# Norms of two heads in one transfer, last head sums split two slots sooner, x added to two output rows in their second phase

## The chip, the cores and the metric

The kernel runs on one core of a Trainium2 chip. The metric is the time of one execution on the device in microseconds; the median of three runs before the change is 1361.49 us (1359.12 to 1362.36). TensorE (PE) multiplies matrices into PSUM banks, VectorE (DVE), ScalarE (ACT) and GpSimd (POOL) work on tiles in SBUF, and SyncE (SP) issues nearly all DMA transfers, which 16 DMA engines carry out. Every engine takes its own instructions in order; semaphores hold one engine until another is done.

## The reference

One layer with two token mixers side by side, for 2048 positions and a model width of 1024, all in float32. The input is normalised and projected once; the projection's six parts feed a gated short convolution (8 heads of 128) and a gated linear recurrence (16 heads of 64). Each head's output is RMS-normalised, multiplied by a SiLU gate, and one output projection and the residual follow.

```python
xn = rms_norm(h, ln_g)
proj = jnp.einsum('bsd,de->bse', xn, w_in)
...
y_conv = headwise_rms_norm(y_conv, N_CONV_HEADS, conv_out_g) * jax.nn.silu(g_conv)
...
y_lru = headwise_rms_norm(y_lru, N_LRU_HEADS, lru_out_g) * jax.nn.silu(g_lru)
y = jnp.concatenate([y_conv, y_lru], axis=-1)
h = h + jnp.einsum('bse,ed->bsd', y, w_out)
return rms_norm(h, final_g)
```

## The kernel before

**Tiles and steps.** The two large products are cut into steps; the table `steps` (line 255) is their order. Steps 0 to 47 are projections of kind `l` (recurrence), `a` and `b` (convolution) for the first half of the positions (h = 0) and the second (h = 1). Steps 48 to 63 are the output projection, kind `o`: phase 0 multiplies the recurrence's heads, phase 1 the convolution's, and each phase has eight tiles m, one for two blocks of 128 rows (rows 2m and 2m + 1). So step 48 + m is phase 0 of tile m and step 56 + m is phase 1 of tile m.

A step computes a 2 x 2 block product with Winograd's variant of Strassen: seven products of sums of blocks. A float32 operand is split into a high part that the fast matmul takes exactly and a low remainder, and each product is three matmuls per block (high x high, high x low, low x high). A step has seven slots (eight where the set of the other operand changes), and a slot has 12 matmuls of 128 x 512 on TensorE. Line 924 is the matmul.

**What sets the order.** The program's order is written by hand. `at(slots, f)` puts f into a list, and `tick()`, called at the start of each slot, runs what has come due: `at(2, f)` runs f two ticks later. The order in which these functions are called is the order of the instructions on each engine. `prep` brings the pieces of the next step's plan, one or two a slot, and `load_next` starts the loads of the step after the next, in slot 3.

**The operands of the output steps.** The gated outputs of the heads lie in DRAM (`yd`), not yet normalised; the norms, one over the root of each head's mean square, lie in DRAM too (`rsd[0]` and `rsd[1]`, one for each half of the positions). `load_z` (line 269) loads four pieces `raw` of `yd`, loads the matching norms into `zr`, broadcast over partitions, and multiplies the two on VectorE. In phase 0 a tile of 128 partitions holds two heads of 64, so the norms of each 64 partitions come from another row, with a transfer of its own (line 285); in phase 1 one row serves all 128 (line 282). From a step that is planned this way, `s_plan` makes sums of the four pieces (VectorE), casts them (ScalarE) and takes the remainders (VectorE).

For four output tiles this is done long before, by the generator `jobs` (line 340), which runs one piece a slot beside the projections of h = 1 and stores the finished operands in DRAM (`so`); when their steps come, they are only loaded (`s<-so`). These are the first two tiles of each phase.

**The head sums.** `finish` (line 617) multiplies gain and gate, stores the product to `yd`, squares the ungated output and calls `head_sums`, in slots counted from the step's last part. After the last head of a half, `head_norms` (line 567) copies the sums to `rt` and its remainder (`split`, ScalarE and VectorE), adds the sums over partitions with four matmuls (`add`, tile `norm_ps`), takes the root (`root`, tile `hn`) and stores the norms in `rsd` (`store`).

**The output.** `outp` (line 837) collects a tile's products in two rows `ob`. In phase 0 it loads the rows of x into `xr`, adds `ob` and stores the sum in DRAM (`od`). In phase 1 it loads `od` back into `xr`, adds, takes the final norm and stores `out`. PSUM has five banks for these products; a bank is free when `q`, `u`, `rr` or `ob` has been copied out of it.

**The queues.** SP issues the transfers in the program's order, and a transfer that waits holds all behind it. Each carries one of a small number of semaphores in turn, so it also waits for an earlier transfer that used the same one.

Of the kernel before, what the change touches and what calls it, by code (L numbers as in the profile page):

```python
# [38 lines left out]
def hymba_kernel(ctx: ExitStack, tc: tile.TileContext, x, xt, w_in, par, lamc, w_gate, w_out, final_g, out):  # L39
# [215 lines left out]
    steps = [(kind, 0, k) for k in range(KT) for kind in "lab"]  # L255
    steps += [(kind, 1, k) for kind, k in zip("lablab", (0, 1, 1, 1, 0, 0))]
    steps += [(kind, 1, k) for k in range(2, KT) for kind in "lab"]
    steps += [("o", ph, m) for ph in range(2) for m in range(KT)]
    cols = {"l": (GLX, GLG), "a": (GC, GX), "b": (GB, GG)}

    def set_of(n):
# [7 lines left out]
    def load_z(h, m, zr, wait):  # L269
        r = [piece("raw") for _ in range(4)]  # L270
        fs = []
        for i in range(2):
            c, b = divmod(2 * m + i, NB)
            assert normed[c // 2]
            rs_ = rsd[c // 2][c % 2]
            zz_, zq_ = [], []
            z2 = wt(("u", "r")[i], "zr") if zr else None

            def norms(dst, k0, n):
                dst = dst.rearrange("p (k t) -> p k t", k=n)  # L280
                if h == 1:
                    nc.sync.dma_start(dst, rs_[b:b + 1, k0:k0 + n, :].broadcast_to((P, n, P)))
                else:
                    for w in range(2):
                        nc.sync.dma_start(dst[w * 64:w * 64 + 64], rs_[b:b + 1, k0 + w * KT:k0 + w * KT + n, :]
                                          .broadcast_to((64, n, P)))

            for q in range(2):
                zz = r[2 * i + q].rearrange("p (k t) -> p k t", k=NB)
                zq = z2[:, q * C:(q + 1) * C] if zr else piece("zr")  # L290
                k0 = (1 - h) * KT + q * NB
                nc.sync.dma_start(zz, yd[c][b, :, k0:k0 + NB, :])
                if not zr:
                    norms(zq, k0, NB)
                elif q == 1:
                    norms(z2, (1 - h) * KT, KT)
                zq = zq.rearrange("p (k t) -> p k t", k=NB)
                fs.append(lambda zz=zz, zq=zq: tt(zz, zz, zq, ALU.mult))
        if wait is not None:
            for i in range(2):  # L300
                at(max(wait + i, 1), *fs[2 * i:2 * i + 2])
        return r, fs
# [19 lines left out]
    def hl_done(n):  # L322
        hlc[0] -= n
# [15 lines left out]

    def jobs():  # L340
        tjobs = [(t, j) for t in (2, 3) for j in range(NB)]
        for ph, m in ((0, 0), (0, 1), (1, 0), (1, 1)):
            (a11, a12, a21, a22), fs = load_z(ph, m, False, None)
            yield from (None,) * 4
            for f in fs[:2]:
                f()
            yield
            for f in fs[2:]:
                f()
            yield  # L350
            if m:
                x_ = aux("s3")
                tt(x_, a11, a21, ALU.subtract)
                tt(a21, a21, a22, ALU.add)
            b = {}

            def blocks():
                if tjobs:
                    b[0] = tjobs.pop(0)
                    b[1] = [piece("traw") for _ in range(4)]  # L360
                    for p, src in zip(b[1], w_blocks(*b[0])):
                        nc.sync.dma_start(p, src)

            def sums():
                if b:
                    b11, b12, b21, b22 = b[1]
                    tt(b11, b12, b11, ALU.subtract)
                    tt(b12, b22, b12, ALU.subtract)

            def more():  # L370
                if b:
                    b11, b12, b21, b22 = b[1]
                    tt(b22, b22, b11, ALU.subtract)
                    tt(b21, b21, b22, ALU.subtract)
                    to = td[b[0]]
                    at(1, lambda: [nc.sync.dma_start(to[n], v) for n, v in enumerate((b22, b11, b12, b21))])
                    b.clear()

            blocks()
            prev = None  # L380
            nothing = lambda: None
            if m:
                items = [(0, a11, lambda: tt(a11, a21, a11, ALU.subtract)), (3, x_, nothing), (2, a21, nothing),
                         (1, a11, nothing), (4, a12, lambda: tt(a12, a12, a11, ALU.subtract)),
                         (6, a22, nothing), (5, a12, nothing)]
            else:
                items = [(n, v, nothing) for n, v in enumerate((a12, a22, a11, a21))]
            for n, (i, v, after) in enumerate(items):
                if prev:
                    prev()  # L390
                    prev = None
                while not may():
                    yield
                t, = hl_tile("so")
                nc.scalar.copy(t[:, 0:C], v)

                def prev(t=t, i=i, v=v, after=after, dst=so[ph, m]):
                    tt(t[:, C:2 * C], v, t[:, 0:C].bitcast(F32), ALU.subtract)
                    after()
                    at(2, lambda: nc.sync.dma_start(  # L400
                        dst[i], t.bitcast(F32).rearrange("p (h c) -> p h c", h=2)))
                    at(3, lambda: hl_done(1))

                yield
            prev()
            made.add((ph, m))
            sums()
            yield
            more()
            yield  # L410
            yield
            blocks()
            yield from (None,) * 4
            sums()
            yield
            more()
            yield from (None,) * 2
# [149 lines left out]
    def head_norms(h):  # L567
        sm_ = sums[0]
        rt, = hl_tile("rt")
        rh, rl = rt[:, 0:C], rt[:, C:2 * C]  # L570
        at(6, lambda: hl_done(1))
        v = {}

        def split():
# [23 lines left out]
            normed[h] = True  # L598

        split()  # L600
        at(3, add)
        at(4, root)
        at(5, lambda: nc.vector.reciprocal(out=v["rs"], in_=v["rs"]))
        at(5, store)

    def head_sums(h, kt, y):
        if summed[0] == 0:
# [4 lines left out]
        summed[0] += 1  # L612
        if summed[0] == 2 * KT:
            summed[0] = 0
            at(1 if h else 7, lambda: head_norms(h))

    def finish(d0, h, kt, y, sil, gain):
        def f1():
# [191 lines left out]
    def conv_b(h, k):  # L810
        g = wt("o2", "gb", bufs=O2)

        def put(which, bank, other):
# [12 lines left out]
                combine(g[:, 0:C] if which == 21 else g[:, C:N2], bank, other)  # L826
            if which == 21:
                silu(g)
                finish(6, h, k, t, g, pt[:, CG + k:CG + k + 1])

        return put

# [4 lines left out]
    def outp(ph, m):  # L837
        ob = [wt("hl", "ob", bufs=HL) for _ in range(2)]
        xr, rest = {}, []
        if ph == 1 and m == 0:  # L840
            fg[0] = wt("t", "fg")
            nc.sync.dma_start(fg[0], final_g.rearrange("(o d) -> o d", o=1).broadcast_to((P, D)))

# [2 lines left out]
            xr[i] = wt("ig", "xr", bufs=IG) if i == 0 else wt("o2", "xr", bufs=O2)  # L846
            nc.sync.dma_start(xr[i], x[tb * P:(tb + 1) * P, :] if ph == 0 else od[tb])

        last = ph == 1 and m == KT - 1
        at(2 if last else 5, lambda: load(0))  # L850
        at(2 if last else 6, lambda: load(1))

        def fin(i):
            tb = 2 * m + i
            if ph == 0:
                at(1, lambda: tt(xr[i], xr[i], ob[i], ALU.add))
                at(3, lambda: nc.sync.dma_start(od[tb], xr[i]))
                return
# [436 lines left out]
```

## Time and profile before

| what | value |
|---|---|
| median of three runs | 1361.49 us |
| the profiled execution's own time | 1361.65 us |
| its span, from the first to the last instruction | 1359.8 us |
| TensorE busy | 1301.9 us |
| VectorE busy | 1032.5 us |
| ScalarE busy | 748.4 us |
| mean DMA rate over the span | 261 GB/s |
| mean granted TensorE clock | 0.989 |

A row of the profile names line, engine and operation, then output tile <- input tiles with their shapes, and how many such instructions there are. In rows in order of time, the first number is the start in us, the second the duration of the group, and a bracket at the end the idle time of the engine before it and what ended it. SPq rows are issues of transfers; their duration is that of the issuing. A row of the waits gives the sum in us, the number of times and the longest. The view of stretches of time gives, for each, the busy time of each engine, the granted clock, the mean busy share of the 16 DMA engines and the rate that they moved. A list of transfers gives their count and the KB of each.

In the profile's clock the output steps start at 1024.5 us (step 48); steps 50, 56 and 63 start at 1072.8, 1191.0 and 1330.4 us.

### The profile page before, as it was taken

To read this page: it belongs to the slowest core of one execution; us is meant where nothing else is said; L and a number is where in the kernel's file an instruction comes from. 1 tells how busy PE (TensorE), PEld (TensorE's weight loads), DVE (VectorE), ACT (ScalarE), POOL (GpSimd) and SP (SyncE) were. 2 spreads that over 40 slices of the span, in tenths; PEclk is the share of its full clock that TensorE was granted. 3 is DMA by queue.
4 is the path that set the end of the run, shared out by engine and by line. 5 is a ranking of instruction groups with operands and counts; after the bars stand their busy time and mean duration, and the time that the engine had idled before them with its cause. 6 is when DMAs were issued, how large, how long until landed. Compare 5 with 4: busy or idle time off the path is not lost.

```text
span 1359.8 us, 16618 instructions
## 1 busy us (share of the span) xinstructions
PE 1301.9 (96%) x5648; PEld 1058.6 (78%) x5648; DVE 1032.5 (76%) x1245; ACT 748.4 (55%) x1139; POOL 226.2 (17%) x160
## 2 busy tenths in 40 slices
PE   6989999999999999899999999999999799998997
PEld 5867877777878787777888888888878688887886
DVE  7778788789989897978566676667458776759885
ACT  7475757575665757565544645364456233444443
POOL 3204242333334340101010110101000000000000
PEclk9989999999999999999999999999999899999999
DMA  7137797988879888542789999999778889797643
GB/s 284 31 119 258 270 252 273 278 296 302 319 281 330 291 291 304 173 162 79 247 304 286 335 354 331 332 339 365 228 253 313 249 236 227 271 404 260 240 146 136
DMA packets 158805, 355.28 MB, mean 261 GB/s; under 512 B 17920, under 2 KB 52736, under 8 KB 158720
## 3 DMA queue, kind: packets, MB, share of 16 engines
q1 hardware_dynamic: 158432, 353.90, 77.1%
q8 instruction: 45, 0.74, 0.2%
q14 instruction: 40, 0.33, 0.1%
q10 hardware_dynamic: 288, 0.32, 0.1%
HBM read 217.11 MB, written 137.04 MB: 260 GB/s over the span
## 4 chain that ended last, share of the span: by engine, by line
PE 40%; DMA 7%; DVE 4%; ACT 3%; issue 1%; SPq 0%; DVEq 0%; ACTq 0%
PE bank L924 40%; DMA traw<-td 1%; DMA zr<-rsd 1%; PE gate L704 1%; ACT i L711 1%; ACT r L711 1%; DVE tl L163 1%; DMA traw<-in_w_out_dram 1%; DMA od<-xr 1%; DMA xr<-od 1%; DVE s L163 1%; DMA xr<-in_x_dram 1%; ACT th L435 1%; DMA yd<-gl 0%; DMA raw<-yd 0%
## 5 line engine op out<-in xcount | busy, mean ns | idle before, releaser
L924 PE MATMUL bank<-th,s 128*128 128x512 f32 x3632 | 1138.8, 392 | 19.9 <-ACT u L1232 10.0
L924 PEld LDWEIGHTS bank<-th,s 128*128 128x128 f32 x3632 | 686.1, 189 | 173.5 <-ACT u L1232 15.0
L924 PE MATMUL bank<-tl,s 128*128 128x512 f32 x1816 | 711.1, 392 | 1.6 <-DVE tl L163 1.3
L924 PEld LDWEIGHTS bank<-tl,s 128*128 128x128 f32 x1816 | 343.2, 189 | 74.8 <-DVE tl L163 3.5
L163 POOL TENSOR_TENSOR s<-raw,s 128x512 fp32r<-128x512 f32 x62 | 110.2, 1790 | 253.9 <-ACT s L200 210.7
L200 ACT CAST s<-raw 128x512 fp32r<-128x512 f32 x140 | 84.5, 616 | 75.4 <-PE bank L924 41.8
L163 DVE TENSOR_TENSOR tl<-traw,th 128x512 fp32r<-128x512 f32 x117 | 85.1, 763 | 40.4 <-ACT th L435 30.0
L1232 ACT COPY u<-bank 128x512 f32<-128x512 f32 x58 | 34.0, 586 | 145.6 <-PE bank L924 77.8
L163 DVE TENSOR_TENSOR s<-s,s 128x512 fp32r<-128x512 f32 x105 | 95.5, 909 | 10.5 <-ACT s L200 10.5
L163 POOL TENSOR_TENSOR gb<-gb,sg 128x1024 f32<-128x1024 f32 x16 | 40.6, 2537 | 348.3 <-ACT sg L637 328.2
L163 DVE TENSOR_TENSOR s<-raw,s 128x512 fp32r<-128x512 f32 (+1 forms) x125 | 92.7, 765 | 6.5 <-ACT s L982 4.4
L200 ACT CAST s<-s 128x512 fp32r<-128x512 f32 x105 | 64.7, 616 | 30.3 <-DVE s L163 25.8
L435 ACT CAST th<-traw 128x512 fp32r<-128x512 f32 x96 | 55.1, 618 | 30.7 <-DMA traw<-td 17.8
L1229 ACT COPY q<-bank 128x512 f32<-128x512 f32 x58 | 33.9, 584 | 68.0 <-PE bank L924 59.2
L678 DVE SCALAR_TENSOR_TENSOR u<-xl,pt,u 128x1024 f32<-128x1024 f32 x48 | 62.7, 1306 | 6.3 <-ACT u L674 5.7
L163 DVE TENSOR_TENSOR raw<-raw,zr 128x512 f32<-128x512 f32 x64 | 41.2, 684 | 34.6 <-DMA zr<-rsd 31.1
L1235 ACT COPY rr<-bank 128x512 f32<-128x512 f32 x58 | 33.8, 583 | 50.4 <-PE bank L924 50.4
L788 DVE SCALAR_TENSOR_TENSOR t<-p,pt,t 128x1024 f32<-128x1024 f32 x32 | 46.5, 1454 | 5.9 <-ACT t L785 5.1
L163 DVE TENSOR_TENSOR st<-u,st 64x1024 fp32r<-64x1024 f32 x32 | 46.5, 1452 | 1.0
L711 ACT ACTIVATE r<-gate,pt 64x512 f32<-64x512 f32 x64 | 43.8, 684 | 3.1 <-PE gate L704 2.4
L163 POOL TENSOR_TENSOR gl<-gl,sg 128x1024 f32<-128x1024 f32 x16 | 40.4, 2523 | 24.5 <-ACT sg L637 24.5
L711 ACT ACTIVATE i<-gate,pt 64x512 f32<-64x512 f32 x64 | 43.8, 684 | 1.1
(153 smaller groups left out, 1153.7 us busy)
## 6 DMA issues: line engine op xcount, KB each, us to landing
sd<-s SPq DMA_DIRECT2D x151, 512.0 KB
s<-sd SPq DMA_DIRECT2D x151, 512.0 KB
raw<-in_w_in_dram SPq DMA_DIRECT2D x104, 256.0 KB
raw<-yd SPq DMA_DIRECT2D x64, 256.0 KB
traw<-in_w_out_dram SPq DMA_DIRECT2D x64, 256.0 KB
so<-so SPq DMA_DIRECT2D x22, 512.0 KB
s<-so SPq DMA_DIRECT2D x22, 512.0 KB
yd<-gl SPq DMA_DIRECT2D x32, 256.0 KB
```

What stands on the lines that cost most here:

```text
L163: (eng or nc.vector).tensor_tensor(out=out, in0=a, in1=b, op=op)
L200: nc.scalar.copy(dst[i][0], val(i))
L435: nc.scalar.copy(self.dst[i, j][0], self.r[i, j])
L678: nc.vector.scalar_tensor_tensor(out=v["u"], in0=o1[:, 1 + j:1 + j + N2], scalar=lw[j], in1=v["u"], op0=ALU.mult, op1=ALU.add)
L704: nc.tensor.matmul(ps[j], v["gw"][n][:, j, :], v["st"][j][:, sl], start=(n == 0), stop=(n == 1))
L711: nc.scalar.activation(out=g_[hi, sl], in_=v["ps"][j][src], func=AF.Sigmoid, bias=pt[src, bias + k:bias + k + 1])
L788: nc.vector.scalar_tensor_tensor(out=tcur["t"], in0=p[:, 2 + j:2 + j + N2], scalar=cw[j], in1=tcur["t"], op0=ALU.mult, op1=ALU.add)
L924: nc.tensor.matmul(bank, a[:, js], b, start=start and n == 0, stop=stop and n == 2, skip_group_check=more)
L1229: nc.scalar.copy(q1, bk["A"])
L1232: nc.scalar.copy(u2, bk["A"])
L1235: nc.scalar.copy(rr, bk["A"])
```

## The change

There are three parts.

1. In `load_z`, the norms of the two heads of a phase 0 tile come with one transfer in place of two. Its DRAM side counts the two heads, then 64 copies, then the row. This holds for steps 50 to 55 (two transfers a step, 512 KB each) and for the tiles (0,0) and (0,1) in `jobs` (four each, 256 KB each).
2. For the second half of the positions, the last `finish` runs a slot sooner and `head_norms` another slot sooner; inside `head_norms` the later parts (`add`, `root`, `store`) are put two slots later, so that they keep their slots.
3. In phase 0 the tiles 0 and 1 store `ob` in `od` without x. In phase 1 these two tiles run last, and their rows of x are loaded there (`xo`) and added to `xr` ahead of `ob`. `jobs` prepares tiles (1,2) and (1,3) in place of (1,0) and (1,1).

```diff
-    steps += [("o", ph, m) for ph in range(2) for m in range(KT)]
+    steps += [("o", 0, m) for m in range(KT)]
+    steps += [("o", 1, m) for m in (2, 3, 4, 5, 6, 7, 0, 1)]
+    X_LATE = (0, 1)
...
-                    for w in range(2):
-                        nc.sync.dma_start(dst[w * 64:w * 64 + 64], rs_[b:b + 1, k0 + w * KT:k0 + w * KT + n, :]
-                                          .broadcast_to((64, n, P)))
+                    src = rs_[b].rearrange("(w k) t -> w k t", k=KT)[1:3, k0 - KT:k0 - KT + n, :]
+                    nc.sync.dma_start(dst, src.unsqueeze(1).broadcast_to((2, 64, n, P)))
...
-        for ph, m in ((0, 0), (0, 1), (1, 0), (1, 1)):
+        for ph, m in ((0, 0), (0, 1), (1, 2), (1, 3)):
...
-        at(6, lambda: hl_done(1))
+        d = 2 if h else 0
+        at(6 + d, lambda: hl_done(1))
...
-        at(3, add)
-        at(4, root)
-        at(5, lambda: nc.vector.reciprocal(out=v["rs"], in_=v["rs"]))
-        at(5, store)
+        at(3 + d, add)
+        at(4 + d, root)
+        at(5 + d, lambda: nc.vector.reciprocal(out=v["rs"], in_=v["rs"]))
+        at(5 + d, store)
...
-            at(1 if h else 7, lambda: head_norms(h))
+            at(0 if h else 7, lambda: head_norms(h))
...
-                finish(6, h, k, t, g, pt[:, CG + k:CG + k + 1])
+                finish(5 if h and k == KT - 1 else 6, h, k, t, g, pt[:, CG + k:CG + k + 1])
...
+        def row(i):
+            xo = wt("o1", "xo", n=N2 + 4)[:, 0:D]
+            tb = 2 * m + i
+            nc.sync.dma_start(xo, x[tb * P:(tb + 1) * P, :])
+            return lambda: tt(xr[i], xr[i], xo, ALU.add)
...
-        last = ph == 1 and m == KT - 1
-        at(2 if last else 5, lambda: load(0))
-        at(2 if last else 6, lambda: load(1))
+        last = ph == 1 and m == 1
+        if ph == 1 and m in X_LATE:
+            add = []
+            order = (1, 0) if last else (0, 1)
+            at(1, lambda: rows(add, order[0]))
+            at(2, lambda: load(order[1]))
+            at(3 if last else 4, lambda: (add[0](), add.append(row(order[1]))))
+            at(5 if last else 7, lambda: add[1]())
+        elif ph == 1 or m not in X_LATE:
+            at(5, lambda: load(0))
+            at(6, lambda: load(1))
...
+            if ph == 0 and m in X_LATE:
+                at(2, lambda: nc.sync.dma_start(od[tb], ob[i]))
+                return
```

Two places show what moves. The first is SP's queue at steps 48 and 49: the loads of step 50 (`raw`, `zr`), then those of step 51, the stores of the last gated rows (`gb`) and of the first output rows (`od`). Before:

```order
L226 DMA s<-so_119 128x1024
L847 DMA xr<-in_x_dram 128x1024
L492 DMA traw<-td_128 128x512
L492 DMA traw<-td_129 128x512
L292 DMA raw<-yd_85 128x512 x2
L285 DMA zr<-rsd_88 64x1024 x2
L292 DMA raw<-yd_85 128x512 x2
L285 DMA zr<-rsd_88 64x1024 x2
L226 DMA s<-so_119 128x1024
```

After the change the same stretch of the queue reads:

```order
L226 DMA s<-so_119 128x1024
L493 DMA traw<-td_128 128x512
L493 DMA traw<-td_129 128x512
L293 DMA raw<-yd_85 128x512 x2
L287 DMA zr<-rsd_88 128x1x1024
L293 DMA raw<-yd_85 128x512 x2
L287 DMA zr<-rsd_88 128x1x1024
L626 DMA yd_86<-gb 128x4x128
L626 DMA yd_87<-gb 128x4x128
L226 DMA s<-so_119 128x1024
```

The load of x is gone from it (another one, a few rows above, too), each pair of norms of 64 rows is one transfer of 128 rows, and the two stores of `gb` stand ahead of the next `s`. A little later in the same queue, at steps 50 and 51, the norms of the second half (`rsd_89`) are stored and the loads of step 52 follow. Before:

```order
L847 DMA xr<-in_x_dram 128x1024 x2
L595 DMA rsd_89<-hn 8x8x32 x12
L857 DMA od_136<-xr 128x1024
L292 DMA raw<-yd_86 128x512 x2
L285 DMA zr<-rsd_89 64x1024 x2
L292 DMA raw<-yd_86 128x512 x2
```

With the change:

```order
L597 DMA rsd_89<-hn 8x8x32 x12
L876 DMA od_136<-ob 128x1024
L876 DMA od_137<-ob 128x1024
L293 DMA raw<-yd_86 128x512 x2
L287 DMA zr<-rsd_89 128x1x1024
L293 DMA raw<-yd_86 128x512 x2
```

Two loads of x are gone, and the second store of tile 1's rows (`od_137`) now stands ahead of step 52's loads. The second place is VectorE at steps 48 and 49, where `sums` become `rt` and step 50's pieces are multiplied. Before:

```order
L163 TENSOR_TENSOR xr<-xr,ob 128x1024
L163 TENSOR_TENSOR tl<-traw,th 128x512 x4
L609 TENSOR_REDUCE sums<-t 128x32
L163 TENSOR_TENSOR raw<-raw,zr 128x512 x2
L163 TENSOR_TENSOR xr<-xr,ob 128x1024
L163 TENSOR_TENSOR tl<-traw,th 128x512 x2
L163 TENSOR_TENSOR raw<-raw,zr 128x512 x2
L163 TENSOR_TENSOR rt<-sums,rt 128x512
```

With the change:

```order
L163 TENSOR_TENSOR tl<-traw,th 128x512 x6
L611 TENSOR_REDUCE sums<-t 128x32
L163 TENSOR_TENSOR rt<-sums,rt 128x512
L163 TENSOR_TENSOR tl<-traw,th 128x512 x2
L163 TENSOR_TENSOR raw<-raw,zr 128x512 x2
L163 TENSOR_TENSOR tl<-traw,th 128x512 x2
L163 TENSOR_TENSOR raw<-raw,zr 128x512 x2
```

`rt` now stands ahead of both pairs of products with `zr`, and the two adds of x and `ob` are gone.

More of the change, by code (lines that the diff above doesn't have):

```diff
@@ L350, in jobs @@
             yield
-            if m:
+            if m % 2:
                 x_ = aux("s3")
@@ L381, in jobs @@
             nothing = lambda: None
-            if m:
+            if m % 2:
                 items = [(0, a11, lambda: tt(a11, a21, a11, ALU.subtract)), (3, x_, nothing), (2, a21, nothing),
@@ L839, in outp @@
         xr, rest = {}, []
-        if ph == 1 and m == 0:
+        if ph == 1 and m == 2:
             fg[0] = wt("t", "fg")
@@ L847, in load, with rows @@
             nc.sync.dma_start(xr[i], x[tb * P:(tb + 1) * P, :] if ph == 0 else od[tb])
-        last = ph == 1 and m == KT - 1
-        at(2 if last else 5, lambda: load(0))
-        at(2 if last else 6, lambda: load(1))
+        def row(i):
[3 more added lines that the diff above has]
+            return lambda: tt(xr[i], xr[i], xo, ALU.add)
+        def rows(first, i):
+            load(i)
+            first.append(row(i))
+        last = ph == 1 and m == 1
[9 more added lines that the diff above has]
+            at(6, lambda: load(1))
         def fin(i):
             tb = 2 * m + i
+            if ph == 0 and m in X_LATE:
+                at(2, lambda: nc.sync.dma_start(od[tb], ob[i]))
+                return
             if ph == 0:
```

## The prediction, made before the changed kernel was run

> **What bounds the kernel now.** I read the page first, then TensorE's waits, the slices of time around the largest of them engine by engine, and last the DMA views.
>
> ```profile
> span 1359.8 us, 16618 instructions
> ...
> PE 1301.9 (96%) x5648; PEld 1058.6 (78%) x5648; DVE 1032.5 (76%) x1245; ACT 748.4 (55%) x1139; POOL 226.2 (17%) x160
> ```
> ```profile
> PE bank L924 <- ACT u L1232: 10.0, 10, 3.8
> ...
> PE norm_ps L582 <- DVE rt L163: 7.1, 1, 7.1
> ```
>
> TensorE is busy for 96% of the span, so a change can win only what is left of its pauses. The largest pause that this change touches is 7.1 us long and happens once: the matmuls of the last head sums wait for `rt`, which VectorE writes. The other row names the second way in which TensorE is held, a copy of `u` by ScalarE. The neighbourhood of the pause, in time:
>
> ```profile
> 1057.14 0.28 PE L582 MATMUL norm_ps<-rt,sel 128*96 128x256 f32 x1
> 1064.53 0.95 PE L582 MATMUL norm_ps<-rt,sel 128*96 128x256 f32 x3 [7.11 <-DVE rt L163]
> ...
> 1066.13 1.05 PE L924 MATMUL bank<-th,s 128*128 128x512 f32 x2
> ...
> 1070.52 0.62 PE L924 MATMUL bank<-th,s 128*128 128x512 f32 x2
> ```
> ```profile
> 1058.12 1.29 DVE L163 TENSOR_TENSOR raw<-raw,zr 128x512 f32<-128x512 f32 x2 [5.38 <-DMA zr<-rsd]
> ...
> 1062.58 1.29 DVE L163 TENSOR_TENSOR raw<-raw,zr 128x512 f32<-128x512 f32 x2 [0.82 <-DMA zr<-rsd]
> 1063.79 0.68 DVE L163 TENSOR_TENSOR rt<-sums,rt 128x512 fp32r<-128x512 f32 x1
> ```
> ```profile
> 1065.88 0.62 ACT L200 CAST s<-s 128x512 fp32r<-128x512 f32 x1 [6.41 <-DVE s L163]
> 1066.40 0.58 ACT L1232 COPY u<-bank 128x512 f32<-128x512 f32 x1
> ```
>
> VectorE takes its work in order. `rt` stands behind two pairs of products raw*zr of step 50, and these wait for the norms `zr` from DRAM. After the pause two matmuls take 1.05 us where they later take 0.62, for about ten matmuls: 2 us more. The pause costs 9 us. The last two rows matter for what comes after it: the copy of `u`, which frees a PSUM bank, stands on ScalarE behind a cast that needs the same products. So the norms' arrival, not `rt` alone, sets the pace here, and the DMA engines are full:
>
> ```profile
> core 0: us, PE busy (x) PEld busy (x) DVE busy (x) ACT busy (x) POOL busy (x), PEclk, DMA share, GB/s
> 714.00:782.00 68.00, 67.78 (x298) 55.49 (x298) 42.89 (x49) 36.73 (x48) 5.91 (x4) 1.00 0.92 310
> 1044.00:1048.00 4.00, 4.00 (x19) 3.34 (x18) 1.55 (x4) 2.68 (x4) 0.00 (x0) 1.00 1.02 374
> 1054.00:1056.00 2.00, 2.00 (x11) 1.59 (x9) 0.00 (x0) 0.69 (x2) 0.00 (x0) 1.00 1.01 224
> 1058.00:1062.00 4.00, 0.00 (x0) 0.00 (x0) 3.63 (x5) 0.62 (x1) 0.00 (x0) 0.67 1.04 234
> 1064.00:1067.00 3.00, 2.47 (x8) 2.08 (x9) 2.97 (x6) 1.11 (x2) 0.00 (x0) 0.50 1.04 422
> 1216.00:1218.00 2.00, 2.00 (x11) 1.65 (x10) 1.09 (x2) 1.27 (x4) 0.00 (x0) 1.00 1.08 398
> ```
>
> All these stretches have a DMA share around 1. Plain transfers of 128 rows move 422 GB/s, 26.4 GB/s for each of 16 engines; the stretches full of the 64-row norms move 224 to 234.
>
> **The transfers of norms: how many engines carry one.** This is the part on which my number rests. Each pair of 64-row transfers becomes one, whose DRAM side counts 2 heads, then 64 copies, then the row; its SBUF side counts 128 rows. The trace shows no such form, but it shows what the leading count does:
>
> ```profile
> DMA packets 158805, 355.28 MB, mean 261 GB/s; under 512 B 17920, under 2 KB 52736, under 8 KB 158720
> ...
> sd<-s SPq DMA_DIRECT2D x151, 512.0 KB
> ...
> rsd<-hn SPq DMA_DIRECT2D x24, 8.0 KB
> ...
> pt<-in_par_dram ACTq DMA_DIRECT2D x1, 52.0 KB
> rsx<-rs SPq DMA_DIRECT2D x2, 2.0 KB
> lam<-in_lam_dram SPq DMA_DIRECT2D x1, 4.0 KB
> ```
>
> The view lists 956 transfers, from the first of these rows to the last. Data pieces under 512 B are few: 24 x 64 of 128 B for `rsd`, 2 x 512 of 4 B for `rsx`, 128 rows each of `pt` and `lam`: 2,816. The other 15,104 small packets belong to no data. They are 16 for each of 932 transfers and 8 for each of the 24 with 8 leading rows: 14,912 + 192 = 15,104, exactly. I read them as one end mark per engine used: 128 and 64 leading rows use 16 engines, 8 use 8. Continued to a leading 2 against 128, an equal cut of both sides gives **2 engines**. The bounds of a 512 KB transfer are then 524,288 / (2 x 26.4) = 9.9 us and 524,288 / 422 = 1.24 us. I take 9.9, because both counts seen obey the same rule.
>
> The Trainium skill, DMA: Bandwidth & Descriptors, section "Why a DMA increments its semaphore by 16 and not by 1", says that the engines of a transfer are the largest number up to 16 that divides both sides' slowest dimension, and that they are always the lowest-numbered ones. The count above agrees for 8, 64 and 128; no run here shows 2. By that page this change's norms would all queue on the same two engines, as the sum below has it.
>
> **The sum at the output steps.** Norms are loaded this way for steps 50 to 55, two transfers each. Every other transfer has a sixteenth of its bytes on each of those two engines and queues there behind the norms (1.24 us for 512 KB, 0.62 for 256).
>
> ```profile
> 1040.93 1.36 SPq L226 DMA_DIRECT2D s<-so  x1
> 1042.38 0.39 SPq L847 DMA_DIRECT2D xr<-in_x_dram  x1
> ...
> 1044.38 0.44 SPq L847 DMA_DIRECT2D xr<-in_x_dram  x1
> ...
> 1157.85 0.32 SPq L857 DMA_DIRECT2D od<-xr  x1
> ```
> ```profile
> 1073.17 1.29 DVE L163 TENSOR_TENSOR raw<-raw,zr 128x512 f32<-128x512 f32 x2 [4.61 <-DMA zr<-rsd]
> ...
> 1078.44 1.22 DVE L163 TENSOR_TENSOR raw<-raw,zr 128x512 f32<-128x512 f32 x2
> ...
> 1083.25 0.69 DVE L163 TENSOR_TENSOR ob<-bank,u 128x512 f32<-128x512 f32 x1
> ...
> 1154.19 1.29 DVE L163 TENSOR_TENSOR raw<-raw,zr 128x512 f32<-128x512 f32 x2 [1.40 <-DMA zr<-rsd]
> ...
> 1159.07 0.68 DVE L163 TENSOR_TENSOR ob<-bank,u 128x512 f32<-128x512 f32 x1
> ```
>
> The `s` load issued at 1040.93 leaves the busy engines near 1043.5. Without the two loads of x, what follows up to step 50's second norms is four `td` halves and one `s` (3.7 us), then twice (two `yd` halves 1.24 + norms 9.9): 22.3; done at 1069.5. Then 6.2 us of `gb`, `s`, `od` and step 51's 22.3: its second norms land at about 1098.5, and the products that began at 1078.44 begin 20 us later.
>
> From there each step repeats. Step 52's loads stand in SP's queue behind `od_137`, which needs `ob<-bank,u`: 4.8 + 0.7 us after those products begin, 1104.0. With 2 us for issue and landing (my estimate: at the end of the run the last 256 KB store shows 3.9 us from issue to the end of the span), 1.24 for `od` and 22.3, step 52 lands at 1129.5. For steps 53 to 55 SP waits for the `od` behind the products: 1157.85 - 1154.19 = 3.7 us. The period is 3.7 + 2 + 1.24 + 22.3 = 29.2 us, against 19.0 now ((1154.19 - 1078.44) / 4). Three periods more: 1217. Before, the same products began at 1154.19. VectorE's `ob<-bank,u`, ScalarE's copy of `u` and the next bank of TensorE stand behind them, so TensorE is **62 us** late, for what was hidden by an earlier start is used up. The lower bound of this term counts only the engine's work, 159.7 us from 1043.5, with no wait for `od`: 50 us. The upper bound adds 2 us of slow matmuls at each of six steps: 74.
>
> **The same transfers earlier.** The norms of tiles (0,0) and (0,1) are loaded much earlier, beside projections (near 661 and 735), now as four 256 KB transfers each instead of eight of 128 KB.
>
> ```profile
> 667.62 3.72 SPq L226 DMA_DIRECT2D s<-sd  x4
> 671.42 0.94 SPq L624 DMA_DIRECT2D yd<-gl  x2
> ```
> ```profile
> 679.13 0.69 DVE L163 TENSOR_TENSOR gl<-bank,rr 128x512 f32<-128x512 f32 x1 [7.74 <-DMA yd<-gl]
> ```
>
> On two engines each takes 131,072 / 26.4 = 5.0 us, 19.9 in all, where 1 MB at 229 GB/s took 4.6: 15.3 more. The stores of `gl` behind them land that much later, and VectorE already waits 7.74 us for them. TensorE's lead of about a slot (2.7 us) and the odd gap absorb some 3; I take 12 us for each tile, 24 together. Bounds: 0, if each load behind them is early enough (a share of 0.92 in 714 to 782 leaves 5 us of room), and 2 x 17, with 2 us of slow matmuls behind each wait.
>
> **The other two parts.** `rt` is written before both pairs of products, and the four adds of x in the first output rows go (1.22 us each). That takes away the 9 us pause, but with late norms the copy of `u` holds TensorE instead; my times above count from before's own clock, so the pause is in them. At the end, four adds and four loads of x are new in the last two steps.
>
> ```profile
> 1339.32 1.29 DVE L868 SCALAR_TENSOR_TENSOR ob<-ob,rs,fg 128x1024 f32<-128x1024 f32 x1
> 1344.84 0.69 DVE L163 TENSOR_TENSOR ob<-bank,rr 128x512 f32<-128x512 f32 x1 [4.23 <-ACT rr L1235]
> ```
>
> The last add stands in this 4.23 us gap: nothing, unless its x row, which waits for the add before it to free the one buffer, comes over 3 us late; then up to 3 us. I take 0, and 0 to 3 as bounds.
>
> **Sum.** The profiled execution took 1361.65 us (span 1359.8 and 1.85 around it), 0.16 above the median 1361.49. 1361.65 + 62 + 24 = 1447.65, **1448 us**. Low: 1361.65 + 50 + 0 = 1412, and 1405 with some microseconds of the landing estimate off; high: 1361.65 + 74 + 34 + 3 = 1473, and 1475.
>
> **Rivals.** (A) *Faster: the merged transfer runs on all 16 engines.* For it: 128-row norms from one DRAM row move at 398 GB/s at 1216. Then the two x loads save 1,048,576 / 374 = 2.8 us; the 8 us near 230 GB/s before step 50's second norms shrink by 3.6, step 51's first by 1.8 more. Its norms come 8.2 us earlier, TensorE resumes behind `ob<-bank,rr` as now, 8.2 us earlier: 1353.4. It decides from the engine count: at 16 it holds, at 8 a transfer takes 2.5 us, about as the pair does now. Against it: the exact count of marks. 13%.
>
> The Trainium skill, SBUF — State Buffer, section "Door 1: The DMA port swizzle", says that 64 partitions from 0 or 64 reach half of the ports. The 224 to 234 against 422 GB/s agree. By it a merged transfer on 16 engines would run at full rate, as in A.
>
> (B) *No change that can be measured:* 16 engines, but the same slow rate; only the 2.8 us of x come off: 1358.9. 4%.
>
> (C) *Two engines, but other ones for each transfer,* so that two norms overlap: 9.9 us off each of the six steps, 1361.65 + 62 - 59 + 24 = 1389. 3%. The forecast has 80%.
>
> **How the numbers follow.** The range 1405 to 1475 is the forecast's own and holds its 80%; A, B and C, 2 in 10, lie outside. A measurement of this kernel can tell about 0.3%, 4.1 us. Slower: 0.80 + 0.03 = 0.83; within 0.3%: 0.04; faster: 0.13.
>
> **What would show it.** Right: the norms' products 25 us and more behind their issue; about 29 us between the products of steps 53, 54 and 55; long waits of VectorE for `zr<-rsd` and, near 680 and 755, for `yd<-gl`; DMA share low in the slices past 1040; `norm_ps` no longer among TensorE's waits; packets under 512 B at 17,920 - 20 x 16 - 20 x 14 = 17,320, for 20 pairs merged and two marks from each merged one. Wrong: norms landing within 10 us, or 17,600 such packets.

## The result and the profile after

The changed kernel takes 1472.28 us (median of 4 runs, 1470.56 to 1472.57) against 1360.3 us before (4 runs, 1357.68 to 1362.36): a ratio of 1.0826, 95% interval 1.0808 to 1.0844. This ratio and those below are the ones on record with their intervals, and can differ by some parts in ten thousand from the quotient of the two medians. It is slower by 8%, forecast at 1448 us. The profiled execution took 1470.56 us.

From the page of the changed kernel: its span, the busy time of each engine, the mean busy share of the 16 DMA engines in 40 slices of 36.7 us with what they moved, and the packets.

```profile
span 1468.7 us, 16601 instructions
...
PE 1318.8 (90%) x5648; PEld 1068.4 (73%) x5648; DVE 1033.1 (70%) x1245; ACT 748.4 (51%) x1139; POOL 226.3 (15%) x160
...
DMA  7148898989898875425967999987853333598764
GB/s 264 28 148 287 226 342 222 328 304 321 285 331 285 296 259 170 156 90 184 346 196 249 351 327 321 359 321 251 262 189 139 126 127 120 170 388 290 250 209 158
DMA packets 158205, 355.28 MB, mean 242 GB/s; under 512 B 17320, under 2 KB 52136, under 8 KB 158120
```

The bytes are the same to the last digit shown and the matmuls are as many, but TensorE is busy for 90% instead of 96%, and for four slices, from about 1100 to 1250 us, the DMA share is at 3 tenths with 120 to 139 GB/s. The packets under 512 B are 17,320, the number that the prediction gave for two engines.

The waits of TensorE after the change, with their sum, their number and the longest:

```profile
PE bank L947 <- ACT u L1255: 62.6, 15, 18.1
PE bank L947 <- DMA s<-sd: 28.0, 2, 16.8
PE bank L947 <- ACT q L1252: 18.9, 9, 6.6
```

`norm_ps` is gone from the list, as forecast. In its place TensorE waits for the copies of `u` and `q` (81.5 us together; before, `u` 10.0 and `q` 7.0) and twice for a load of `s`. Busy time by stretch, with the granted clock, the DMA share and GB/s in the last three columns, after the change:

```profile
1040.00:1260.00 220.00, 154.08 (x607) 122.51 (x606) 100.75 (x142) 65.17 (x107) 3.27 (x1) 0.85 0.46 156
1208.00:1216.00 8.00, 8.00 (x37) 6.61 (x36) 0.69 (x1) 2.31 (x4) 0.00 (x0) 1.00 0.13 52
```

and before, over a stretch in which TensorE is busy for about as long:

```profile
1040.00:1200.00 160.00, 152.26 (x661) 124.94 (x660) 114.25 (x166) 60.84 (x106) 0.00 (x0) 0.97 0.88 266
```

The DMA share of the output steps has fallen to about half, and the rate from 266 to 156 GB/s. The stretch from 1208 to 1216 holds norms alone: a share of 0.13 is 2 of 16 engines, and 52 GB/s are 26 for each of the two. What VectorE then waits for, in time:

```profile
1132.08 1.29 DVE L163 TENSOR_TENSOR raw<-raw,zr 128x512 f32<-128x512 f32 x2 [6.13 <-DMA zr<-rsd]
...
1153.87 1.29 DVE L163 TENSOR_TENSOR raw<-raw,zr 128x512 f32<-128x512 f32 x2 [12.20 <-DMA zr<-rsd]
...
1165.84 1.29 DVE L163 TENSOR_TENSOR raw<-raw,zr 128x512 f32<-128x512 f32 x2 [8.87 <-DMA zr<-rsd]
...
1185.80 1.30 DVE L163 TENSOR_TENSOR raw<-raw,zr 128x512 f32<-128x512 f32 x2 [7.05 <-DMA zr<-rsd]
...
1197.62 1.29 DVE L163 TENSOR_TENSOR raw<-raw,zr 128x512 f32<-128x512 f32 x2 [8.72 <-DMA zr<-rsd]
```

These are the second products of step 51 and both of steps 52 and 53: 33.8 and 31.8 us from step to step, where the forecast had 31 and 29.2. SyncE's issues of `od` between them:

```profile
1169.50 0.33 SPq L880 DMA_DIRECT2D od<-xr  x1
...
1201.28 0.32 SPq L880 DMA_DIRECT2D od<-xr  x1
```

`od` follows the products by 3.7 us in both cases, as forecast; the next step's norms are queued behind it. The other place, near 680 and 770 us, on TensorE:

```profile
684.17 0.77 PE L947 MATMUL bank<-th,s 128*128 128x512 f32 x1 [11.25 <-DMA s<-sd]
```
```profile
774.73 0.79 PE L947 MATMUL bank<-th,s 128*128 128x512 f32 x1 [16.75 <-DMA s<-sd]
```

Here plain loads of `s`, which have nothing to do with the norms, arrive late. I read it so that a sixteenth of each stands behind the norms on each of the two engines; this follows from the order of the queue, for the trace does not say which engine carried a packet.

### The profile page after: what moved, and what is told of

Read it like the earlier page. It is cut to its first block, busy times and chain, and to the rows that moved or that the text cites. A ratio compares the mean times of both kernels' runs of the same rounds, so it can differ in the third digit from the quotient of the medians.

```text
span 1468.7 us, 16601 instructions
## 1 busy us (share of the span) xinstructions
PE 1318.8 (90%) x5648; PEld 1068.4 (73%) x5648; DVE 1033.1 (70%) x1245; ACT 748.4 (51%) x1139; POOL 226.3 (15%) x160
## 2 busy tenths in 40 slices
DMA packets 158205, 355.28 MB, mean 242 GB/s; under 512 B 17320, under 2 KB 52136, under 8 KB 158120
## 4 chain that ended last, share of the span: by engine, by line
PE 32%; DMA 17%; DVE 5%; ACT 3%; issue 1%; SPq 1%; DVEq 0%; ACTq 0%
PE bank L947 31%; DMA zr<-rsd 11%; DVE s L163 2%; DMA yd<-gl 1%; DMA s<-sd 1%; DVE raw L163 1%; DMA traw<-td 1%; DMA s<-so 1%; PE gate L706 1%; ACT i L713 1%; ACT r L713 1%; DMA xr<-od 1%; DMA xr<-in_x_dram 0%; DVE ob L163 0%; SPq L293 0%
## 5 line engine op out<-in xcount | busy, mean ns | idle before, releaser
L947 PE MATMUL bank<-th,s 128*128 128x512 f32 x3632 | 1152.4, 396 | 120.0 <-ACT u L1255 62.6
L947 PEld LDWEIGHTS bank<-th,s 128*128 128x128 f32 x3632 | 693.5, 191 | 279.9 <-ACT u L1255 69.2
L947 PEld LDWEIGHTS bank<-tl,s 128*128 128x128 f32 x1816 | 346.8, 191 | 75.3 <-DVE tl L163 3.0
L1258 ACT COPY rr<-bank 128x512 f32<-128x512 f32 x58 | 33.8, 583 | 70.0 <-PE bank L947 70.0
```

What stands on the lines that cost most here:

```text
L947: nc.tensor.matmul(bank, a[:, js], b, start=start and n == 0, stop=stop and n == 2, skip_group_check=more)
L1258: nc.scalar.copy(rr, bk["A"])
```

## Experiments

The theory T is that all of the loss comes from the merged transfers, because a leading count of 2 puts them on two engines. The rivals: the other two parts have a share in it; or the merged form is slow for another reason than its engine count.

**1. Pairs again.** The changed kernel with part one undone.

```diff
-                    src = rs_[b].rearrange("(w k) t -> w k t", k=KT)[1:3, k0 - KT:k0 - KT + n, :]
-                    nc.sync.dma_start(dst, src.unsqueeze(1).broadcast_to((2, 64, n, P)))
+                    for w in range(2):
+                        nc.sync.dma_start(dst[w * 64:w * 64 + 64], rs_[b:b + 1, k0 + w * KT:k0 + w * KT + n, :]
+                                          .broadcast_to((64, n, P)))
```

> The changed kernel with the norms of ph 0 as two 64-row transfers again, so that only the last head sums and the x rows are moved. T (all of the loss comes from the merged transfers, which run on two DMA engines): 1352 to 1359 us, the pause of 7.1 us for rt gone and nothing lost. R1 (the moved sums or the x rows bring part of the loss): above 1366 us, and by as much the loss of the merged kernel is not the transfers'.

Measured: 1356.43 us against 1358.18 before, ratio 0.9993 (0.9983 to 1.0003). The loss is gone, all of it. But the pause of 7.1 us has gone too, and nothing that can be measured was won. VectorE in this kernel, at the place of the old pause:

```profile
1044.05 0.69 DVE L163 TENSOR_TENSOR rt<-sums,rt 128x512 fp32r<-128x512 f32 x1 [0.65 <-ACT rt L578]
1051.39 1.29 DVE L163 TENSOR_TENSOR raw<-raw,zr 128x512 f32<-128x512 f32 x2 [5.46 <-DMA zr<-rsd]
...
1065.84 1.29 DVE L163 TENSOR_TENSOR raw<-raw,zr 128x512 f32<-128x512 f32 x2 [5.31 <-DMA zr<-rsd]
```

and TensorE behind it:

```profile
1059.01 0.59 PE L948 MATMUL bank<-th,s 128*128 128x512 f32 x1 [2.97 <-ACT u L1256]
1068.99 0.50 PE L948 MATMUL bank<-th,s 128*128 128x512 f32 x1 [2.64 <-DVE ob L163]
```

`rt` is now written well ahead of the products, and TensorE still waits: twice, for 5.6 us together, behind products that wait for norms. Counted from the start of step 48 (1024.5 us before, 1020.0 here), step 50's products come only 2.2 and 3.1 us sooner than before, about the 2.8 us that the prediction put on the two loads of x. One wait was replaced by two.

**2. The merge alone, and at one place at a time.** The kernel before with part one and nothing else; and the changed kernel with the merge only for the early tiles, or only for the output steps (`elif zr:` in the place of `elif not zr:`):

```diff
-                else:
+                elif not zr:
                     src = rs_[b].rearrange("(w k) t -> w k t", k=KT)[1:3, k0 - KT:k0 - KT + n, :]
                     nc.sync.dma_start(dst, src.unsqueeze(1).broadcast_to((2, 64, n, P)))
+                else:
+                    for w in range(2):
+                        nc.sync.dma_start(dst[w * 64:w * 64 + 64], rs_[b:b + 1, k0 + w * KT:k0 + w * KT + n, :]
+                                          .broadcast_to((64, n, P)))
```

> The kernel before with the merged transfers and nothing else. T: 1460 to 1485 us, no better than the changed kernel, since the pause for rt then lies under the longer wait for the norms; packets under 512 B 17,320. R1: below 1440 us.

> The changed kernel with merged transfers only for tiles (0,0) and (0,1), which are loaded beside the projections; the output steps keep their pairs. T: the two stalls seen in the changed kernel (11.4 + 2.2 and 16.9 + 3.0 us) are the price of eight transfers of 256 KB on two engines: the time of the kernel with pairs only, some 1356, and 33.5 us: 1390, between 1380 and 1396. If the prediction's 24 us was right and the rest of the stalls came from the output steps' state: 1380 or less.

> The changed kernel with merged transfers only for output steps 50 to 55; tiles (0,0) and (0,1) keep their pairs. T: the terms add up, so 1472.3 - 33.5 = 1439 us, between 1430 and 1445, with a period of 32 to 33 us between the products of steps 53, 54 and 55. If the two places help each other (work that comes late early leaves a smaller backlog later): 1448 or more. If the prediction's 62 us was right for this term: 1356 + 62 = 1418.

Measured: merge alone 1472.72 us, ratio 1.085 (1.0828 to 1.0872), the same as the whole change. Early tiles only: 1387.29, ratio 1.022 (1.0198 to 1.0241), 30.9 us over the kernel with pairs. Output steps only: 1439.38, ratio 1.0603 (1.0581 to 1.0626), 83.0 over it. 30.9 + 83.0 = 113.9, and the whole change lies 115.9 over the kernel with pairs: the two terms add up, and neither is 24 or 62.

The traces say the same by stage. From the start of TensorE's matmuls in each, in us:

| kernel | step 48 starts at | steps 48 to 55 take | step 56 to the end |
|---|---|---|---|
| before | 1024.5 | 166.5 | 168.8 |
| pairs | 1020.0 | 164.9 | 169.1 |
| merge at the early tiles only | 1050.4 | 164.3 | 170.0 |
| merge at the output steps only | 1018.7 | 248.5 | 170.5 |
| the change | 1052.7 | 247.9 | 168.1 |

The merged transfers cost the output steps 82 us against before, and nothing behind them beyond 2 us. The first column holds one more thing: the profiled execution before reaches step 48 later than those of the kernels with pairs at the early tiles, by 4.5 and 5.8 us. At 650 us, ahead of the first loads that differ, it is already 4.2 and 5.6: executions differ by that much.

So the times of the kernel with the merge at the output steps alone have to be moved before they are laid beside the prediction's own, which count from before's clock. SyncE issues the same two stores, before and in this kernel, at

```profile
1038.76 0.97 SPq L624 DMA_DIRECT2D yd<-gl  x2
```
```profile
1032.91 0.97 SPq L630 DMA_DIRECT2D yd<-gl  x2
```

5.8 us apart. Second products of its steps 50 to 55:

```profile
1069.32 1.29 DVE L163 TENSOR_TENSOR raw<-raw,zr 128x512 f32<-128x512 f32 x2 [9.64 <-DMA zr<-rsd]
...
1098.86 1.29 DVE L163 TENSOR_TENSOR raw<-raw,zr 128x512 f32<-128x512 f32 x2 [6.41 <-DMA zr<-rsd]
...
1132.52 1.29 DVE L163 TENSOR_TENSOR raw<-raw,zr 128x512 f32<-128x512 f32 x2 [8.72 <-DMA zr<-rsd]
...
1164.32 1.29 DVE L163 TENSOR_TENSOR raw<-raw,zr 128x512 f32<-128x512 f32 x2 [8.72 <-DMA zr<-rsd]
...
1196.68 1.29 DVE L163 TENSOR_TENSOR raw<-raw,zr 128x512 f32<-128x512 f32 x2 [8.78 <-DMA zr<-rsd]
...
1228.69 1.29 DVE L163 TENSOR_TENSOR raw<-raw,zr 128x512 f32<-128x512 f32 x2 [8.67 <-DMA zr<-rsd]
```

With 5.8 us added they are 1075.1, 1104.7, 1138.3, 1170.1, 1202.5 and 1234.5. Forecast were 1069.5, 1098.5, 1129.5, 1158.7, 1187.9 and 1217. The first two come 5.6 and 6.2 us late; from there each step takes 2.6 to 3.2 us longer than the forecast's 31 and 29.2.

**3. Other leading counts.** Each norms row of ph 0 is stored several times over in a second DRAM tensor, so that the merged transfer's source leads with 16, 8 or 4 rows. The bytes that reach SBUF, the destination and the number of transfers of norms stay; four copies from DRAM to DRAM come on top. `RE` is 8, 4 and 2 for leading counts of 16, 8 and 4.

```diff
+    RE = 8
+    rse = [dram.tile([2, NB, 2 * RE, KT, P], F32, name=f"rse{h}") for h in range(2)]
...
+            for w in range(2):
+                nc.sync.dma_start(
+                    rse[h].rearrange("i b (w e) k t -> w (i b) e (k t)", w=2)[w],
+                    rsd[h].rearrange("i b (w k) t -> w (i b) (k t)", w=3)[w + 1].unsqueeze(1)
+                    .broadcast_to((2 * NB, RE, KT * P)))
...
-                    src = rs_[b].rearrange("(w k) t -> w k t", k=KT)[1:3, k0 - KT:k0 - KT + n, :]
-                    nc.sync.dma_start(dst, src.unsqueeze(1).broadcast_to((2, 64, n, P)))
+                    src = rse[c // 2][c % 2, b][:, k0 - KT:k0 - KT + n, :]
+                    nc.sync.dma_start(dst, src.unsqueeze(1).broadcast_to((2 * RE, 64 // RE, n, P)))
```

> The changed kernel, but each norms row of ph 0 is stored eight times over in DRAM (two copies from DRAM to DRAM of 256 KB for each half of the norms), so that the merged transfer's source counts 16 rows, then 8 copies, then the row; bytes, destination and number of transfers are those of the changed kernel. T (engines follow from the leading count): 16 engines, 512 KB in 1.24 to 2.3 us, the loss gone: 1348 to 1357 us. R2 (the form is slow, one transfer over both heads with the copies as an inner count, whatever leads it): about 1472 us. R3 (16 engines, but no better than the pairs' rate): as the kernel with pairs, 1354 to 1359 us.

> The same with each row stored four times, so that the leading count is 8. T: 8 engines, 524288 / (8 x 26.4) = 2.5 us for a transfer, near the 2.3 us of a pair; measured period less the time saved, 28.1 - 2 x 7.4 + 3.7 = 17 us, is under the 18 us that the step takes with pairs: 1353 to 1361 us. R2: about 1472.

> The same with each row stored twice, so that the leading count is 4. T: 4 engines, 524288 / (4 x 26.4) = 5.0 us for a transfer; the period between the norms' products is then 28.1 - 2 x 5.0 + 3.7 = 21.9 us against 18 with pairs, some 20 us over the steps, and up to 5 at each of tiles (0,0) and (0,1): 1381, between 1365 and 1392 us. R2: about 1472.

Measured: 16 rows 1361.62 us, ratio 1.0021 (1.0009 to 1.0033); 8 rows 1379.94, ratio 1.0153 (1.0118 to 1.0188); 4 rows 1404.35, ratio 1.0333 (1.0303 to 1.0362); and 2 rows, the change itself, 1472.28. The rival that the form is equally slow whatever leads it is out. The packets of the kernels with 16, 8 and 4 rows:

```profile
DMA packets 158773, 356.33 MB, mean 261 GB/s; under 512 B 17632, under 2 KB 52448, under 8 KB 158688
```
```profile
DMA packets 158485, 355.80 MB, mean 258 GB/s; under 512 B 17472, under 2 KB 52288, under 8 KB 158400
```
```profile
DMA packets 158341, 355.54 MB, mean 254 GB/s; under 512 B 17392, under 2 KB 52208, under 8 KB 158256
```

With 16, 8 and 4 end marks for each merged transfer in place of 32 for a pair, and 8 for each of the four copies, the prediction's count gives 17,920 - 20 x 16 + 32 = 17,632, 17,920 - 20 x 24 + 32 = 17,472 and 17,920 - 20 x 28 + 32 = 17,392: exact three times. A stretch of the 4-row kernel that holds norms alone, and two of the 16-row kernel, the first with these norms and, in its second half, loads of `yd`, the second with plain loads:

```profile
1190.00:1196.00 6.00, 6.00 (x28) 4.95 (x28) 3.05 (x6) 2.35 (x4) 0.00 (x0) 1.00 0.26 106
```
```profile
1052.00:1054.00 2.00, 2.00 (x10) 1.66 (x9) 0.00 (x0) 0.24 (x1) 0.00 (x0) 1.00 1.01 244
1212.00:1218.00 6.00, 6.00 (x28) 4.99 (x27) 3.51 (x5) 3.91 (x8) 0.00 (x0) 1.00 1.03 397
```

Four engines: a share of 0.26 and 106 GB/s, 26.5 for each, twice the 52 of two engines. (The 8-row kernel: 0.49 and 197 GB/s from 1174 to 1177 us.) Sixteen engines: a share of 1, but 244 GB/s, 15.3 for each; a norms packet of 4 KB takes 0.27 us there (the median), where it takes 0.16 on 2, 4 or 8 engines. So T holds for the engine count, and the third theory of the expectation (16 engines, no better than the pairs' rate) holds for the rate. The times of the 4-row and 8-row kernels missed my figures, by 12 and 19 us at the upper end, and the 16-row kernel lies 3 us above the third theory's range. Up to 4 us may be the storing of the copies, if one takes the 16-row kernel's excess over the pairs for it (ratios 1.0021 and 0.9993). By stage, the 4-row kernel starts step 48 18 us behind the kernel with pairs and takes 30 us more for steps 48 to 55, where the expectation had up to 10 and some 20; for 8 rows it is 9 and 17, where it had no loss.

**4. The same 16-row norms without the other two parts.**

> The kernel before with the 16-row norms and nothing else of the change: the head sums and the x rows stand as before. If the norms' arrival sets the pace near 1060 us (as the kernel with pairs suggests, whose gain of 7.7 us there is given back within five slots): faster than before by some microseconds, 1350 to 1357 us, and the wait of norm_ps for rt shorter than 7.1 us. If the order of rt sets it: no better than before, 1356 to 1361 us, and clearly above the 16-row norms with both other parts.

Measured: 1363.96 us, ratio 1.004 (1.0023 to 1.0056). The condition of this experiment, norms that arrive sooner, was not met (244 GB/s above): `norm_ps` still waits 6.3 us for `rt`, behind products that still wait for `zr`. So it does not tell the two apart and was inconclusive; the time lies above both ranges.

**5. The two heads from two queues.** The kernel with pairs, with the second transfer of each pair from ScalarE:

```diff
-                        nc.sync.dma_start(dst[w * 64:w * 64 + 64], rs_[b:b + 1, k0 + w * KT:k0 + w * KT + n, :]
+                        (nc.sync, nc.scalar)[w].dma_start(dst[w * 64:w * 64 + 64], rs_[b:b + 1, k0 + w * KT:k0 + w * KT + n, :]
```

> The kernel with pairs, but the second head's 64-row transfer of each pair is issued by ScalarE instead of SyncE, so that the two heads of a tile can be under way at once. If two transfers on the two halves of the partitions overlap: stretches full of norms near 400 GB/s, the norms of steps 50 to 55 up to 2 us earlier each, some 8 us off near 1060 as rival A had it: 1346 to 1353 us. If they share one path: as with pairs, 1353 to 1360. If ScalarE's issues wait for buffers in front of its casts: above 1362.

Measured: 1363.85 us, ratio 1.0032 (1.0018 to 1.0047). It is slightly slower. The issues of step 50's norms on the two engines' queues:

```profile
1042.51 0.45 ACTq L287 DMA_DIRECT2D zr<-rsd  x1
...
1046.12 0.45 ACTq L287 DMA_DIRECT2D zr<-rsd  x1
...
1052.69 0.45 SPq L287 DMA_DIRECT2D zr<-rsd  x1
...
1055.38 0.45 SPq L287 DMA_DIRECT2D zr<-rsd  x1
```

ScalarE issues its two 10 and 9 us ahead of SyncE's, which stand behind other transfers, so the two heads of this step were hardly under way at once. At step 53 the two queues' issues lie within 3 us, and the stretch from 1109 to 1112 us moves 238 GB/s at a DMA share of 1.00: no sign of an overlap at full rate, though `yd` halves are among the transfers. Most of the loss lies elsewhere, in the third branch of the expectation. At tile (0,1), ScalarE's issues stand ahead of its copy of `rr`, and TensorE waits for that copy:

```profile
728.64 7.57 ACTq L287 DMA_DIRECT2D zr<-rsd  x3
736.31 0.58 ACT L1259 COPY rr<-bank 128x512 f32<-128x512 f32 x1 [8.37 <-DMA zr<-rsd]
```
```profile
736.94 0.79 PE L948 MATMUL bank<-th,s 128*128 128x512 f32 x1 [4.80 <-ACT rr L1259]
```

**6. Why 16 engines were no faster.** The kernel with pairs, with other transfers in the 16-by-8 form: those of `od`, whose 128 rows are all different.

```diff
-    od = [dram.tile([P, D], F32, name=f"od{b}") for b in range(S // P)]
+    od = [dram.tile([16, 9, D], F32, name=f"od{b}")[:, 0:8, :] for b in range(S // P)]
```

> The kernel with pairs, but each block of od lies in DRAM as 16 groups of 8 rows with one unused row behind each group, so that its stores and loads count 16, then 8, then the row, as the norms with 16 stored rows do, while every row is another one and all 128 partitions take part. Theory P (16 engines that each write 8 neighbouring partitions get in each other's way on the SBUF side): the packets of od take some 0.27 us instead of 0.16, 240 GB/s. Theory D (it is the DRAM side, one row read again and again): 0.16 us and about 400 GB/s. The time is of less interest: 1354 to 1368 us.

Measured: 1363.67 us, ratio 1.0031 (1.0016 to 1.0046). Two stretches of this kernel, the first ahead of its first loads of `od`, the second among them:

```profile
1196.00:1206.00 10.00, 10.00 (x46) 8.29 (x45) 4.02 (x6) 4.05 (x8) 0.00 (x0) 1.00 1.04 407
1208.00:1211.00 3.00, 3.00 (x15) 2.49 (x14) 0.00 (x0) 1.34 (x3) 0.00 (x0) 1.00 1.03 220
```

and the kernel with pairs, which loads `od` as 128 plain rows from 1199.73 on:

```profile
1196.00:1206.00 10.00, 10.00 (x45) 8.27 (x45) 4.05 (x6) 6.22 (x11) 0.00 (x0) 1.00 1.03 407
1208.00:1218.00 10.00, 10.00 (x45) 8.29 (x45) 5.71 (x10) 5.07 (x10) 0.00 (x0) 1.00 1.03 399
```

Rows that are read once each are slowed just as much by the form alone (220 against 399 to 407 GB/s, all engines busy in both); their packets take 0.28 us (the median) instead of 0.16, as theory P had it. So it isn't that one DRAM row is read again and again: theory D is out, and P is borne out as far as the form goes. Another cause on the DRAM side isn't excluded, for the form also changes which DRAM rows are moved at the same time.

**7. The other two parts, one by one.** The kernel with pairs, with the order of the output rows and the x rows put back (sums alone), or with the three delays of the head sums put back (x alone):

```diff
-            at(0 if h else 7, lambda: head_norms(h))
+            at(1 if h else 7, lambda: head_norms(h))
...
-        d = 2 if h else 0
+        d = 0
...
-                finish(5 if h and k == KT - 1 else 6, h, k, t, g, pt[:, CG + k:CG + k + 1])
+                finish(6, h, k, t, g, pt[:, CG + k:CG + k + 1])
```

> The kernel before with only the last head sums split two slots sooner. If the norms set the pace near 1060 us whatever the order of rt: no difference that can be measured, 1354 to 1361 us. If the sums win something that the x rows give back: 1350 or less.

> The kernel before with only the x rows of the first two output rows moved to their second phase. If the end hides its four loads and four adds and the two loads of x saved near 1044 us are hidden by the norms: no difference that can be measured, 1354 to 1361 us. If the end costs something that the sums win back: 1362 or more.

Measured: sums alone 1358.11 us, ratio 0.9997 (0.9983 to 1.0011); x rows alone 1357.01, ratio 0.9982 (0.9971 to 0.9993). Neither wins or costs anything that is worth a line; the x rows alone, at 1 to 3 parts in a thousand, have the lowest ratio of the study, but their interval overlaps that of the kernel with pairs.

## Why the prediction was right, and where its sum fell short

- **Two engines: right.** The count of small packets was 17,320 as forecast, the stretch from 1208 to 1216 shows 2 of 16 engines at 26 GB/s each, and the count follows the leading number at 16, 8 and 4 as well. The sentence of the Trainium skill, DMA: Bandwidth & Descriptors, section "Why a DMA increments its semaphore by 16 and not by 1", is borne out in the number of engines at a leading 2, of which the trace before had no transfer. That transfers queue on the same ones is shown by the time: with two engines of its own for each transfer (rival C) the products of a step would not lie 11.8 us apart (1185.80 to 1197.62).
- **The output steps: mechanism right, the size too small.** The term was 62 us. The kernel with the merge there takes 82.0 us more for steps 48 to 55 than before (248.5 against 166.5), 8 beyond the term's upper bound of 74. By the second products of step 55 it is 17.5 us behind the forecast: 5.6 of these are there at step 50, 0.6 come at step 51, and 2.6 to 3.2 at each of the four steps behind. Of the 5.6, 2.1 lie ahead of the norms, whose first packet starts at 1044.7, 1050.5 on before's clock, where the sum has 1048.4; the rest comes in the transfers and the landing. In a period, the 3.7 us up to `od` were right. The sum gave 2 + 1.24 + 22.3 = 25.5 us from `od` to the second products; the changed kernel took 1197.62 - 1169.50 = 28.1. The transfers behind `od` in that kernel:

```profile
1169.50:1170.30 0.80, 0.00 (x0) 0.00 (x0) 0.77 (x2) 0.00 (x0) 0.00 (x0) 0.84 0.00 0
1170.30:1171.50 1.20, 0.00 (x0) 0.00 (x0) 1.17 (x3) 0.00 (x0) 0.00 (x0) 0.50 1.05 389
1171.50:1174.20 2.70, 2.05 (x5) 1.66 (x6) 2.70 (x4) 1.10 (x2) 0.00 (x0) 0.50 0.91 224
```

For 0.8 us nothing moves. `od` follows at 389 GB/s, but the two `yd` halves behind it at 224, and the first packet of the norms starts at 1174.19: 3.9 us where the sum had 2.5. By the trace's packets, the later of the first norms' two end marks comes at 1185.29, after 11.1 us instead of 9.9, and the next two halves with the second norms take 11.85 instead of 11.14. From the last end mark to the products it is 0.5 us. So "2 us for issue and landing (my estimate)" was too much (0.8 + 0.5 = 1.3), and the step that failed is the price of the transfers themselves, each at the full 26.4 GB/s of an engine. Alone that nearly holds (524,288 / 52 GB/s = 10.1 us against 9.9); just behind the `yd` halves the norms' first packets take up to 0.32 us instead of 0.16. Why they do stays open.
- **The early tiles: mechanism right, the size too small.** 24 us forecast, 30.9 measured alone. The two stalls are 11.25 and 16.75 us in the changed kernel, 28.0 together: the second alone is nearly 5 us over the 12 that I gave each tile. Behind each stall the matmuls are slower for 5 to 6 us (two in 1.05 us instead of 0.62). I had priced them through VectorE's wait for `yd<-gl`, with 3 us taken off for TensorE's lead; what TensorE waited for last were loads of `s` behind the norms. The upper bound of 34 covered it.
- **The pause: right.** The forecast let it vanish and gave nothing for it, as the norms' arrival sets the pace. The kernel with pairs shows just that, without the merge's disturbance: no wait for `rt`, two new ones, and a time that differs by no more than the noise.
- **The end: right.** The four late loads and adds of x cost nothing that can be measured (x alone, 0.9982).
- **Rivals.** A (16 engines, full rate, 1353.4) fails twice: the transfer runs on two engines, and the kernel with 16 rows shows that on 16 engines this form does not reach the full rate. The row on which A rested, 1216 to 1218 us, holds almost only packets of 2 KB, those of `yd` halves; the 128-row norms, 4 KB a row, follow it, at about the same rate (406 GB/s from 1217.8 to 1219.0). Had the count been 16, B's rate would have been the right one. With it falls what the prediction drew from the Trainium skill, SBUF — State Buffer, section "Door 1: The DMA port swizzle", for this case: the 16-row transfer spans all 128 partitions and still moves 244 GB/s.

With 82.0 and 30.9 in their places the sum is 1361.65 + 82.0 + 30.9 = 1474.6, 2.3 us above the median; the base, a single profiled execution, was itself 1.4 us above the 1360.3 of the kernel before. That the time lies inside the range, under 3 us from its end, owes something to luck: both terms were short, and one went beyond its own bound. The other's bound of 34 and the 3 us for the end left room for it.

## What to carry to other kernels

Before two DMAs are made into one, look at the leading count of both sides: here 2, 4, 8 and 16 in front gave as many engines, and a broadcast over two rows leads with 2, however many copies follow. The count of small packets on the page tells the engine count without a run of the new form, and a DMA share of 0.13 (2 of 16) in a stretch in which everything waits is its mark afterwards; other transfers pay as well: here plain loads of `s` held TensorE for 28 us. And a pause that names one late operand is worth nothing if the next operand on the same engine is just as late: see what would be waited for next before you move the first.

## What the runs showed of the hardware beyond that

A transfer to all 128 partitions on all 16 engines can still run at little more than half rate. In the form of 16 groups of 8 rows it moved 244 GB/s (norms) and 220 (`od`), with the DMA share at 1, where plain transfers of 128 rows moved 397 to 407 in the same kernels. Its neighbours are slowed with it: packets of 2 KB took 0.14 us (norms) and 0.15 (`od`) beside it, 0.085 elsewhere. The Trainium skill, DMA: Bandwidth & Descriptors, section "The descriptor swizzle", says that a transfer of 128 partitions is dealt out so that each engine writes to one port of its own. If the 16-by-8 form instead gives each engine eight neighbouring partitions, engines that start together would meet at the same ports; no run here shows which partitions an engine wrote, so this stays an argument.
